# Output projection of a hybrid decoder layer by Strassen's scheme on pairs of row blocks, with the layer norm in steps between the products

## The chip, the cores and the metric

The kernel runs on 1 core of one Trainium2 chip. The metric is the device time of one execution in microseconds (us); a run of the kernel before was timed three times. PE is TensorE, DVE VectorE, ACT ScalarE, POOL GpSimd and SP SyncE, which issues the DMAs here.

## The reference, cut to what matters

One decoder layer on 4096 rows of 1024 columns in float32. One input projection feeds two branches of 512 columns each: sliding-window attention (`out_a`) and gated linear attention (`out_b`). Both are joined, projected by `w_out` (1024 x 1024), added to the input and normalised:

```
proj = jnp.einsum('bsd,de->bse', x, w_in[layer])
...
mix = jnp.einsum('bse,ed->bsd', jnp.concatenate([out_a, out_b], axis=-1), w_out[layer])
x = layer_norm(ALPHA * x + mix, ln_g[layer], ln_b[layer])
```

`layer_norm` takes mean and variance over the 1024 columns of a row, then multiplies by `ln_g` and adds `ln_b`.

## The kernel before

The rows are cut into 32 blocks of 128. Three stages follow each other on one core. **Stage A** projects a block for the attention branch, runs the sliding-window attention and writes the branch's transposed output (`att`, 128x512) to DRAM (`mixd[n][0]`). **Stage B** does the same for the linear-attention branch: per block the projections `bq`, `bv`, `bk`, `bg`, then the chunked recurrence. `b_state` (L537 to L553) scales the running state `tot` by a decay into `st` (DVE, L546) and splits it into `sbh` (ACT, L550) and `sbl` (POOL, L551); the products of `b_out` (L658 to L660) need both. `b_sums` forms `qp` on POOL (L532), which `b_turn` transposes (`tb`, L564). `b_store` (L680 to L687) transposes the block's output, copies it (`mb`) and writes it to `mixd[n][1]`. **Stage C** is the output projection and the layer norm.

All large products are made from float32 operands split in a high and a low part, so that one product is three matmuls: high by high, high by low, low by high. `split` (L97 to L105) makes the parts, ACT the high one (L100, a cast), DVE or POOL the low one (L105, a subtract). `project` (L127 to L137) issues the three matmuls of each of the 8 pieces of the contraction (lines L135, L136, L137), 128x512 each.

Per block stage C loads the two halves of the mix (`mr`) and the input rows (`xr`), splits `mr` into `mh`, `ml`, and makes two halves of 24 matmuls into PSUM (`py`). DVE reads each half (L761), takes its statistics (L762, L763) and works out the scale (L785 to L790, with two short ACT steps, and L776); ACT normalises the 128x1024 tile (L777), POOL multiplies by `ln_g` (L778), DVE adds `ln_b` (L779), and SP writes the rows out. The last block takes a shorter way (L771 to L773).

The program is written block by block, but a tile scheduler sets the order of the instructions on each engine from the tiles' dependences; an engine then works through its list in that order and waits at each instruction for its inputs and for its output's place to come free. Where a list puts an instruction that waits ahead of one that could go, the second waits too. SP's list of DMA issues is such a list as well. The output weights `w_o` are loaded and split at the last block of stage B (`load_group`, L112 to L121) into the places of the input weights.

## Time and profile before

| what | value |
|---|---|
| median of 3 runs | 1723.22 us (1723.13 to 1724.64) |
| the profiled execution's own time | 1724.99 us |
| its span | 1723.3 us |
| mean granted TensorE clock | 0.996 |
| PE busy | 1691.6 us, 98% |
| DVE busy | 1122.5 us, 65% |
| ACT busy | 774.2 us, 45% |
| POOL busy | 498.2 us, 29% |
| moved by DMA | 119.68 MB, mean 69 GB/s |

The span is the time from the first to the last instruction of one profiled execution; its busy shares are averages over the three stages, of which A ends at about 675 us, B at about 1358 us and C at the end. The granted clock is the share of TensorE's full speed that the throttle allowed: 1.00 is 2.4 GHz, and the lower of the two levels, 1.2 GHz, shows as a lower mean in a stretch.

### The profile page before, as it was taken

The page shows a single profiled execution, that of the slowest core. Times are in us where ns is not written, and L with a number is a line of the kernel's source. Part 1 is how long each engine was busy: PE and PEld are TensorE (multiplying, and loading weights), DVE is VectorE, ACT ScalarE, POOL GpSimd, SP SyncE. Part 2 cuts the span into 40 slices and gives each one's busy share as a digit, 9 for nine tenths or more (in the row PEclk, how much of TensorE's full clock was granted, in tenths as well). Part 3 has the DMA queues.
Part 4 walks back from the last instruction along what each step waited for, and adds up shares of the span by engine and source line. Part 5 has one row for each costly group of instructions (what it writes and reads, how often), then busy time and mean ns, then how long its engine had stood idle before and what let it go on. Part 6 is the DMA issues. An engine that isn't in the chain of part 4 may idle for free.

```text
span 1723.3 us, 26109 instructions
## 1 busy us (share of the span) xinstructions
PE 1691.6 (98%) x9466; PEld 1444.3 (84%) x9466; DVE 1122.5 (65%) x2547; ACT 774.2 (45%) x2064; POOL 498.2 (29%) x634
## 2 busy tenths in 40 slices
PE   7999999999999999999999999999999899999998
PEld 5788888888888887888888888888888788888886
DVE  6877777777777786666666666666665655555555
ACT  5444434444444455555555555555555522222221
POOL 3333322333222355222222222222222422222221
PEclk9999999999999999999999999999999899999999
DMA  6211111111111132111111111111111444444442
GB/s 197 80 38 37 37 46 47 37 38 38 37 53 40 37 102 79 50 38 38 38 38 38 38 38 38 38 38 38 38 37 38 153 146 143 142 144 146 147 147 86
DMA packets 65525, 119.68 MB, mean 69 GB/s; under 512 B 22642, under 2 KB 26100, under 8 KB 65396
## 3 DMA queue, kind: packets, MB, share of 16 engines
q1 hardware_dynamic: 65396, 118.01, 21.2%
q8 instruction: 74, 1.21, 0.3%
q14 instruction: 55, 0.45, 0.1%
HBM read 84.37 MB, written 33.62 MB: 68 GB/s over the span
## 4 chain that ended last, share of the span: by engine, by line
PE 58%; DVE 1%; ACT 1%; issue 0%; DMA 0%; POOL 0%; DVEq 0%; POOLq 0%; ACTq 0%
PE py L135 7%; PE py L137 7%; PE py L136 7%; PE bg L135 3%; PE bg L137 3%; PE bg L136 3%; PE bv L135 3%; PE bv L136 3%; PE bv L137 3%; PE bq L135 2%; PE bq L136 2%; PE bq L137 2%; PE bk L137 2%; PE bk L136 2%; PE bk L135 2%; PE to L684 1%
## 5 line engine op out<-in xcount | busy, mean ns | idle before, releaser
L361 POOL TENSOR_SCALAR_AFFINE_SELECT p<-hl 128x512 fp32r<-128x512 f32 x256 | 165.6, 682 | 382.7 <-ACT hl L355 348.8
L135 PE MATMUL py<-wh,mh 128*128 128x512 f32 x512 | 200.3, 391 | 0.0
L136 PE MATMUL py<-wl,mh 128*128 128x512 f32 x512 | 200.1, 391 | 0.0
L137 PE MATMUL py<-wh,ml 128*128 128x512 f32 x512 | 200.1, 391 | 0.0
L330 ACT ACTIVATE pr<-psc,ngm 128x128 f32<-128x128 f32 x256 | 90.7, 367 | 193.8 <-PE psc L311 138.1
L778 POOL TENSOR_TENSOR y<-y,lg 128x1024 f32<-128x1024 f32 x31 | 74.2, 2394 | 269.0 <-ACT y L777 253.5
L532 POOL TENSOR_TENSOR qp<-bqs,ee 128x256 f32<-128x256 f32 x32 | 23.6, 738 | 337.3 <-ACT ee L529 323.9
L137 PEld LDWEIGHTS py<-wh,ml 128*128 128x128 f32 x512 | 96.7, 189 | 20.3
L135 PEld LDWEIGHTS py<-wh,mh 128*128 128x128 f32 x512 | 96.7, 189 | 20.0
L136 PEld LDWEIGHTS py<-wl,mh 128*128 128x128 f32 x512 | 96.7, 189 | 19.8
L135 PE MATMUL pq<-wh,xh 128*128 128x512 f32 x256 | 105.0, 410 | 7.4 <-ACT wh L100 6.3
L135 PE MATMUL pg<-wh,xh 128*128 128x512 f32 x256 | 110.5, 433 | 0.1
L135 PE MATMUL bg<-wh,xh 128*128 128x512 f32 x256 | 107.0, 418 | 0.0
L137 PE MATMUL pq<-wh,xl 128*128 128x512 f32 x256 | 102.6, 401 | 1.2 <-DVE xl L105 1.2
L135 PE MATMUL bv<-wh,xh 128*128 128x512 f32 x256 | 103.5, 404 | 0.0
L100 ACT CAST mh<-mr 128x1024 fp32r<-128x1024 f32 x32 | 33.7, 1054 | 154.2 <-PE py L136 154.2
L105 DVE TENSOR_TENSOR xl<-xraw,xh 128x512 fp32r<-128x512 f32 x128 | 94.7, 760 | 11.6 <-ACT xh L100 5.2
L136 PE MATMUL pq<-wl,xh 128*128 128x512 f32 x256 | 102.1, 399 | 0.1
L136 PE MATMUL pg<-wl,xh 128*128 128x512 f32 x256 | 100.6, 393 | 1.3 <-POOL wl L105 1.0
L137 PE MATMUL pg<-wh,xl 128*128 128x512 f32 x256 | 101.0, 395 | 0.0
L136 PE MATMUL bv<-wl,xh 128*128 128x512 f32 x256 | 100.9, 394 | 0.0
L137 PE MATMUL bg<-wh,xl 128*128 128x512 f32 x256 | 100.7, 393 | 0.0
(221 smaller groups left out, 4907.1 us busy)
## 6 DMA issues: line engine op xcount, KB each, us to landing
xraw<-in_xt_dram SPq DMA_DIRECT2D x64, 512.0 KB
mr<-mx SPq DMA_DIRECT2D x64, 256.0 KB
xr<-in_xn_dram SPq DMA_DIRECT2D x32, 512.0 KB
out_dram<-y SPq DMA_DIRECT2D x31, 512.0 KB
mx<-att SPq DMA_DIRECT2D x32, 256.0 KB
mx<-mb SPq DMA_DIRECT2D x32, 256.0 KB
wraw<-in_w_a_dram SPq DMA_DIRECT2D x16, 256.0 KB
wraw<-in_w_b_dram SPq DMA_DIRECT2D x16, 256.0 KB
```

Source lines behind the costliest of these rows:

```text
L100: act.copy(hdst, src)
L105: leng.tensor_tensor(ldst, src, hdst, ALU.subtract)
L135: pe.matmul(dst[:, :n], a, hs[k][:, :n], start=(k == 0), stop=False)
L136: pe.matmul(dst[:, :n], a, ls[k][:, :n], start=False, stop=False)
L137: pe.matmul(dst[:, :n], b, hs[k][:, :n], start=False, stop=(k == NK - 1))
L330: act.activation(pr[:, i], sc[i], AF.Exp, bias=ngm[:, h : h + 1], scale=0.125, accum_out=den[:, h : h + 1])
L361: pool.affine_select(o, hl[:, i], [[0, 4], [sg_, P]], ALU.is_gt if b else ALU.is_ge, 0.0, base=0, channel_multiplier=-sg_,)
L532: pool.tensor_tensor(qp, B[n]["q"], ee, ALU.mult)
L684: pe.transpose(to[:, hs], og[:, hs], ident)
L778: pool.tensor_tensor(y, y, lg, ALU.mult)
```

## The change

Two blocks make a pair. Let `a11`, `a21` be the halves of the two blocks that come from stage A (even block, odd block) and `a12`, `a22` those from stage B. Instead of the eight half-products of 12 matmuls for a pair, seven products of sums and differences are made (the Strassen-Winograd form): 7 products of 4 pieces by 3 matmuls, 84 for a pair where there were 96.

The seven left operands of a pair are kept in DRAM (`opd[p][0..6]`). Four of them are sums, made on DVE in `b_store` of the odd block (L702, L704, L707, L709 of the changed kernel, 128x512 each). The seven combinations of `w_o` are made by `w_prepare` in small pieces during stage B, split there, written to DRAM (`wod`) and fetched by `w_fetch` at the turn from B to C: 28 tiles of 512 KB, where before 16 tiles of 256 KB were read. The `q` and `k` weights of stage B become one group of 528 columns, and some buffers of stage B lose their second copy or share a place (`gw`, `og`, `qp`, `kp`, `r0`).

In stage C `step(p, t)` makes product t of pair p into one of three PSUM banks (a, b, a, c, a, b, a), and DVE reads the bank after each product; a product that adds to a bank cannot begin before that read. Operands are loaded two pairs ahead and split one pair ahead, one between two steps (`split_op`, L855 and L856). `normed` is the layer norm of one block as a generator that is pushed on between the products: statistics, scale, `Identity` on ACT (L901), the multiplication by `ln_g` on POOL in two halves (L904), then the addition of `ln_b` in two halves (L908), on POOL for an even block, on DVE for an odd one. Pairs 0 and 1 are interleaved, the others go one by one. The small products of the scale have a scalar operand in place of a second tile.

```diff
--- before.py
+++ after.py
...
-    mixd = [
-        [dr.tile([P, 4, P], F32, tag=f"mx{n}_{h}", name=f"mx{n}_{h}") for h in range(2)]
-        for n in range(NB)
+    opd = [
+        [dr.tile([P, 512], F32, tag=f"op{p}_{i}", name=f"op{p}_{i}") for i in range(7)]
+        for p in range(NB // 2)
+    ]
...
+            p, odd = divmod(n, 2)
+            a2 = b1.tile([P, 512], F32, tag=f"mb{odd}", name=f"mb{n}")
+            act.copy(a2, to)
+            sp.dma_start(opd[p][4 + odd], a2)
+            if not odd:
+                a11 = b1.tile([P, 512], F32, tag="a11", name=f"a11_{p}")
+                a21 = b1.tile([P, 512], F32, tag="a21", name=f"a21_{p}")
+                sp.dma_start(a11, opd[p][0])
+                sp.dma_start(a21, a21d[p])
+                B[n]["a"] = a11, a21, a2
+                return
+            a11, a21, a12 = B[n - 1]["a"]
+            dve.tensor_tensor(a11, a11, a21, ALU.subtract)
+            sp.dma_start(opd[p][2], a11)
+            dve.tensor_tensor(a21, a21, a2, ALU.add)
+            sp.dma_start(opd[p][3], a21)
+            s2 = b1.tile([P, 4, P], F32, tag="om", name=f"s2_{p}").rearrange("p a s -> p (a s)")
+            dve.tensor_tensor(s2, a2, a11, ALU.subtract)
+            sp.dma_start(opd[p][1], s2)
+            dve.tensor_tensor(a12, a12, s2, ALU.subtract)
+            sp.dma_start(opd[p][6], a12)
...
+        def w_prepare(k, c):
+            q = []
+            for i in range(2):
+                for j in range(2):
+                    r = wr.tile([P, 256], F32, tag="wraw", name=f"wo{k}_{c}{i}{j}")
+                    sp.dma_start(r, w_o[k + 4 * i, :, 512 * j + 256 * c : 512 * j + 256 * c + 256])
+                    q.append(r)
...
+            def part(i, src):
+                w = b2.tile([P, 2, 256], F32R, tag="wo", name=f"wop{i}_{k}{c}")
+                split(w[:, 0], w[:, 1], src, act, dve)
+                sp.dma_start(wod[i][k][:, :, 256 * c : 256 * c + 256], w.bitcast(F32))
+            yield
+            part(0, r11)
+            dve.tensor_tensor(r11, r12, r11, ALU.subtract)
+            yield
+            dve.tensor_tensor(r12, r22, r12, ALU.subtract)
+            part(6, r22)
...
+        def op_places(p):
+            a = xp.tile([P, NK, P], F32, tag="xraw", name=f"oa{p}").rearrange("p a s -> p (a s)").bitcast(F32R)
+            b = xp.tile([P, NK, P], F32R, tag="xh", name=f"ob{p}").rearrange("p a s -> p (a s)")
+            c = xp.tile([P, NK, P], F32R, tag="xl", name=f"oc{p}").rearrange("p a s -> p (a s)")
+            w = {0: (b[:, LO], a[:, LO]), 3: (b[:, HI], a[:, HI]), 1: (c[:, LO], c[:, HI])}
+            for i in w:
+                op_load(p, w, i)
+            return w
+        PLACE = {0: (0, 0), 3: (0, 4), 1: (1, 0), 4: (1, 4), 2: (2, 0), 6: (2, 4)}
+        def w_fetch(i, pool_=None):
+            for k in range(4):
+                if pool_ is None:
+                    slot, k0 = PLACE[i]
+                    w = wp.tile([P, 2, 528 if slot == 1 else 512], F32R, tag=f"w{slot}_{k0 + k}", name=f"wo{i}_{k}")
+                else:
+                    w = pool_.tile([P, 2, 512], F32R, tag=f"wo{k}", name=f"wo{i}_{k}")
+                sp.dma_start(w[:, :, :512].bitcast(F32), wod[i][k])
+                wo[i][k] = w
...
             if last:
-                wo[0] = load_group(wr, w_o, 0, 512, 0, 512)
+                w_fetch(0)
+                w_fetch(3)
+            next(prep, None)
             pk = bank("pj", f"bk{n}")
-            project(pk, x, wb["k"], 256)
+            project(pk, x, wb["qk"], 256, off=272)
+            if last:
+                w_fetch(1)
+                w_fetch(4)
...
+            next(prep, None)
             if last:
-                wo[1] = load_group(wr, w_o, 512, 512, 2, 512)
+                ops = [op_places(p) for p in range(2)]
+                w_fetch(2)
+                w_fetch(6)
+            if n == NB - 2:
+                for _ in prep:
+                    pass
...
+        def op_more(p, w, which=(4, 2, 6, 5)):
+            for i in which:
+                h = c2.tile([P, 512], F32R, tag=f"oh{i}", name=f"oh{i}_{p}")
+                l = c2.tile([P, 512], F32R, tag=f"ol{i}", name=f"ol{i}_{p}")
+                w[i] = h, l
+                op_load(p, w, i)
...
+        def split_op(w, i):
+            h, l = w[i]
+            act.copy(h, l.bitcast(F32))
+            dve.tensor_tensor(l, l.bitcast(F32), h, ALU.subtract)
+        def product(dst, w, i, more=False):
+            h_, l_ = w[i]
+            for k in range(4):
+                h, l = wo[i][k][:, 0, :512], wo[i][k][:, 1, :512]
+                a, b = h_[:, k * P : (k + 1) * P], l_[:, k * P : (k + 1) * P]
+                pe.matmul(dst, a, h, start=(not more and k == 0), stop=False, skip_group_check=more)
+                pe.matmul(dst, a, l, start=False, stop=False, skip_group_check=more)
+                pe.matmul(dst, b, h, start=False, stop=(k == 3), skip_group_check=more)
...
+        def normed(n, y, st, late, tail):
...
+            dve.bn_aggr(mv, st.rearrange("p a b -> p (a b)"))
+            dve.tensor_scalar(ms, ms, 1.0, EPS, ALU.mult, ALU.add)
+            log_(rs, ms)
+            act.activation(rs, rs, AF.Exp, scale=-0.5)
+            yield
+            dve.tensor_scalar(nt, rs, rs, -0.5, ALU.mult, ALU.mult)
+            dve.tensor_scalar(nt, nt, ms, 1.5, ALU.mult, ALU.add)
+            dve.tensor_scalar(r2, nt, rs, None, ALU.mult)
+            rows = slice(n * P, (n + 1) * P)
+            if tail:
+                for s in (LO, HI):
+                    dve.scalar_tensor_tensor(y[:, s], y[:, s], mv[:, 0:1], lg[:, s], ALU.subtract, ALU.mult)
+                    dve.scalar_tensor_tensor(y[:, s], y[:, s], r2, lb[:, s], ALU.mult, ALU.add)
+                    sp.dma_start(out[rows, s], y[:, s])
+                return
...
+            nb_ = c2.tile([P, 1], F32, tag=f"nb{n % 2}", name=f"nb{n}")
+            dve.tensor_scalar(nb_, mv[:, 0:1], r2, -1.0, ALU.mult, ALU.mult)
+            act.activation(y, y, AF.Identity, bias=nb_, scale=r2)
+            yield
+            for s in (LO, HI):
+                pool.tensor_tensor(y[:, s], y[:, s], lg[:, s], ALU.mult)
+            if late is dve:
+                yield
+            for s in (LO, HI):
+                late.tensor_tensor(y[:, s], y[:, s], lb[:, s], ALU.add)
+            sp.dma_start(out[rows, :], y)
...
+        for p in range(2):
+            op_more(p, ops[p])
+        ys = [load_rows(p) for p in range(2)]
+        w_fetch(5, c1)
...
-            for i in range(2):
-                s = slice(512 * i, 512 * i + 512)
-                py = bank(("pj", "tp")[n % 2], f"py{n}_{i}")
-                project(py, (mh, ml), wo[i], 512)
-                dve.scalar_tensor_tensor(y[:, s], xr[:, s], ALPHA, py, ALU.mult, ALU.add)
-                dve.bn_stats(st[:, i, :], y[:, s])
...
-            dve.scalar_tensor_tensor(nb_, mv[:, 0:1], -1.0, rs, ALU.mult, ALU.mult)
-            act.activation(y, y, AF.Identity, bias=nb_, scale=rs)
-            pool.tensor_tensor(y, y, lg, ALU.mult)
-            dve.tensor_tensor(y, y, lb, ALU.add)
...
+        for i in ORDER:
+            for p in range(2):
+                split_op(ops[p], i)
+        pairs, later = NB // 2, []
+        def run_later():
+            for g in list(later):
+                if next(g, 0) == 0:
+                    later.remove(g)
...
+        STEPS = (("a", 0, False), ("b", 3, False), ("a", 1, True), ("c", 4, False), ("a", 2, True), ("b", 6, True), ("a", 5, True))
+        READS = ((0, 0, True), (1, 1, True), (0, 1, True), (0, 0, False), (1, 1, False), (0, 1, False), (1, 0, True))
+        state = {}
+        def step(p, t):
+            if t == 0:
+                b = {x: bank(g, f"p{x}{p}") for x, g in (("a", "pj"), ("b", "c"), ("c", "d"))}
+                st = [c2.tile([P, 2, 6], F32, tag=f"st{i}", name=f"cst{2 * p + i}") for i in range(2)]
+                state[p] = b, st
+            b, st = state[p]
+            x, op, more = STEPS[t]
+            product(b[x], ops[p], op, more)
+            i, half, first = READS[t]
+            y, s = ys[p][i], (LO, HI)[half]
+            if first:
+                dve.scalar_tensor_tensor(y[:, s], y[:, s], ALPHA, b[x], ALU.mult, ALU.add)
+            else:
+                dve.tensor_tensor(y[:, s], y[:, s], b[x], ALU.add)
+            if t in (3, 4, 5, 6):
+                dve.bn_stats(st[i][:, half, :], y[:, s])
+            run_later()
+            if t in (5, 6):
+                g = normed(2 * p + i, y, st[i], (pool, dve)[i], p == pairs - 1 and i == 1)
+                next(g)
+                later.append(g)
...
+        for group in [(0, 1)] + [(p,) for p in range(2, pairs)]:
+            for t in range(7):
+                for p in group:
+                    step(p, t)
+                    if p + 2 < pairs and t == 2:
+                        ops[p + 2] = op_places(p + 2)
+                    elif p + 2 < pairs and t > 2:
+                        op_more(p + 2, ops[p + 2], ORDER[t : t + 1])
+                nxt = group[-1] + 1
+                if nxt == pairs:
+                    continue
+                if t == 4:
+                    ys[nxt] = load_rows(nxt)
+                ready = range(7)[t : t + 1] if nxt > 2 else ((), (), (), (), (0, 1, 2), (3,), (4, 5, 6))[t]
+                for i in ready:
+                    split_op(ops[nxt], ORDER[i])
+        while later:
+            run_later()
```

**VectorE, stage B, block 20.** `am` is the masked attention tile of the block, `st` the scaled state, `r4` a small helper of the next block, `al` a low part, `tot` the running state, `a11`, `a21` the operands of the pair before. Before:

```order
L630 TENSOR_TENSOR gw20_13066<-bg20_12996,nrm_396 128x512
L590 COPY_PREDICATED am0_7814<-cs_373,pat20_13095 128x512
L546 TENSOR_SCALAR st20_13110<-tot19_12890,dd20_13107 128x128 x2
L482 TENSOR_TENSOR r41_399<-bq21_13082,r41_399 128x2x16
L105 TENSOR_TENSOR al20_13104<-am0_7814,ah20_13103 128x512
L612 TENSOR_TENSOR tot20_13144<-pu20_13137,st20_13110 64x256 x2
```

The change:

```order
L595 COPY_PREDICATED am0_7810<-cs_441,pat20_13372 128x512
L546 TENSOR_TENSOR dd20_13384<-sm20_13277,sm19_13010 128x2
L702 TENSOR_TENSOR a11_10_13563<-a11_10_13563,a21_10_13564 128x512
L488 TENSOR_TENSOR r41_467<-bq21_13359,r41_467 128x2x16
L112 TENSOR_TENSOR al20_13381<-am0_7810,ah20_13380 128x512
L551 TENSOR_SCALAR st20_13387<-tot19_13148,dd20_13384 128x128 x2
L617 TENSOR_TENSOR tot20_13421<-pu20_13414,st20_13387 64x256 x2
```

`st` stood right behind `am`; now the subtract of a pair's operands, the helper and the low part `al` stand between them. The same order is there in blocks 6, 8, up to 28; in the odd blocks `st` stands behind `am` and `dd` as before.

**VectorE, stage C, end of pair 8 and begin of pair 9** (blocks 16 to 19). `pa9` and `pb9` are banks of pair 9, `ol`, `oh` low and high parts of operands of the next pair, `nb` and `cnt` scale terms, `y17` the odd block of pair 8. Before, around the same block:

```order
L761 SCALAR_TENSOR_TENSOR y16_17354<-xr16_17348,py16_0_17357 128x512
L779 TENSOR_TENSOR y15_17273<-y15_17273,lb_16046 128x1024
L762 BN_STATS cst16_17355<-y16_17354 128x6
L761 SCALAR_TENSOR_TENSOR y16_17354<-xr16_17348,py16_1_17384 128x512
L762 BN_STATS cst16_17355<-y16_17354 128x6
```

The change:

```order
L948 SCALAR_TENSOR_TENSOR y18_17978<-y18_17978,pa9_18044 128x512
L856 TENSOR_TENSOR ol5_10_18040<-ol5_10_18040,oh5_10_18039 128x512
L889 TENSOR_SCALAR cnt17_18033<-crs17_18032 128x1
L890 TENSOR_SCALAR cnt17_18033<-cnt17_18033,mv17_18031 128x1
L891 TENSOR_SCALAR cr217_18034<-cnt17_18033,crs17_18032 128x1
L900 TENSOR_SCALAR nb17_18070<-mv17_18031,cr217_18034 128x1
L948 SCALAR_TENSOR_TENSOR y19_17980<-y19_17980,pb9_18045 128x512
L908 TENSOR_TENSOR y17_17806<-y17_17806,lb_16481 128x512 x2
L948 SCALAR_TENSOR_TENSOR y18_17978<-y18_17978,pa9_18044 128x512
L856 TENSOR_TENSOR oa11_18108<-oa11_18108,ob11_18109 128x512 x2
L950 TENSOR_TENSOR y18_17978<-y18_17978,pc9_18046 128x512
```

The addition of `ln_b` to `y` of the block before (L779) stood between the two reads of a block; it now stands as L908 ahead of the second read of bank `pa9`. The same is there for the ends of pairs 2, 4, 5, 7, 8, 10, 11, 13 and 14; at the other ends L908 stands right behind that read.

**SP, the turn from stage B to stage C.** `wo` are the weights of stage C, `sd31` and `sm31` the two ends of a small transfer through DRAM that the state of block 31 needs, `ol4_0` an operand of pair 0, `y0` the input rows of block 0. Before:

```order
L520 DMA sd31_164<-r031_15840 1x256
L521 DMA sd31_164<-r131_15841 1x256
L687 DMA mx30_1_130<-mb30_15861 128x512
L112 DMA wraw2_4_15932<-in_w_o_dram 128x512
L112 DMA wraw2_5_15938<-in_w_o_dram 128x512
L524 DMA sm31_15846<-sd31_164 128x4x1
```

The change:

```order
L781 DMA wo4_2_16228<-wod4_2_215 128x2x512
L781 DMA wo4_3_16230<-wod4_3_216 128x2x512
L526 DMA sd31_256<-r031_16242 1x256
L527 DMA sd31_256<-r131_16243 1x256
L693 DMA op15_4_178<-mb30_16261 128x512
L760 DMA oc1_16320<-op1_1_77 128x512
L781 DMA wo2_0_16324<-wod2_0_205 128x1024
L530 DMA sm31_16248<-sd31_256 128x4x1
...
L760 DMA ol4_0_16441<-op0_4_73 128x512
...
L872 DMA y0_16464<-in_xn_dram 128x1024
```

`sd31` stood behind 13 weight tiles of 256 KB; it now stands behind 16 of 512 KB, one more of them stands between it and `sm31`, and 25 further transfers stand ahead of the input rows of block 0.

## Rows read from the trace of the kernel before

**Rows 1.** The page's first part: busy time, share of the span, instructions.

```profile
PE 1691.6 (98%) x9466; PEld 1444.3 (84%) x9466; DVE 1122.5 (65%) x2547; ACT 774.2 (45%) x2064; POOL 498.2 (29%) x634
```

**Rows 2.** The chain that ended last, shares of the span.

```profile
PE 58%; DVE 1%; ACT 1%; issue 0%; DMA 0%; POOL 0%; DVEq 0%; POOLq 0%; ACTq 0%
```

**Rows 3.** Windows: from:to, length, busy us of PE PEld DVE ACT POOL, PEclk, DMA, GB/s.

```profile
750.00:1300.00 550.00, 550.00 (x3421) 485.40 (x3420) 333.09 (x796) 302.55 (x743) 139.81 (x178) 1.00 0.13 38
1410.00:1700.00 290.00, 290.00 (x1281) 240.14 (x1280) 158.34 (x322) 73.00 (x108) 63.36 (x27) 1.00 0.42 143
```

**Rows 4.** Timeline of PE, stage C: start, length (us), engine, line, operation.

```profile
1700.03 0.39 PE L135 MATMUL py<-wh,mh 128*128 128x512 f32 x1
1700.26 0.39 PE L136 MATMUL py<-wl,mh 128*128 128x512 f32 x1
```

**Rows 5.** Timeline of DVE, stage C: first reads of two blocks, one block between.

```profile
1590.07 0.69 DVE L761 SCALAR_TENSOR_TENSOR y<-xr,py 128x512 f32<-128x512 f32 x1 [1.34 <-PE py L137]
...
1611.83 0.69 DVE L761 SCALAR_TENSOR_TENSOR y<-xr,py 128x512 f32<-128x512 f32 x1 [1.35 <-PE py L137]
```

**Rows 6.** Groups of stage C, 1410 to 1700 us: busy us, mean ns, idle before.

```profile
L761 DVE SCALAR_TENSOR_TENSOR y<-xr,py 128x512 f32<-128x512 f32 x54 | 37.1, 687 | 68.1 <-PE py L137 68.1
...
L779 DVE TENSOR_TENSOR y<-y,lb 128x1024 f32<-128x1024 f32 x26 | 31.9, 1226 | 45.5 <-POOL y L778 45.5
...
L778 POOL TENSOR_TENSOR y<-y,lg 128x1024 f32<-128x1024 f32 x27 | 64.6, 2394 | 229.1 <-ACT y L777 229.1
...
L777 ACT ACTIVATE y<-y,nb,crs 128x1024 f32<-128x1024 f32 x27 | 33.6, 1244 | 21.9 <-DVE nb L776 21.9
```

**Rows 7.** Groups of stage B, shapes apart: a POOL multiply.

```profile
L636 POOL TENSOR_TENSOR gw<-gw,gs 128x512 f32<-128x512 f32 x26 | 33.7, 1298 | 75.2 <-ACT r L481 75.2
```

**Rows 8.** Timeline of one block of stage B: DVE, ACT, POOL, PE.

```profile
1074.60 0.73 DVE L590 COPY_PREDICATED am<-cs,pat 128x512 f32<-128x512 uint32 x1
1075.22 1.19 DVE L546 TENSOR_SCALAR st<-tot,dd 128x128 f32<-128x128 f32 x2
...
1076.43 0.68 DVE L105 TENSOR_TENSOR al<-am,ah 128x512 fp32r<-128x512 f32 x1
...
1076.44 0.83 ACT L550 CAST sbh<-st 64x256 fp32r<-64x256 f32 x2 [0.46 <-DVE st L546]
...
1074.83 1.30 POOL L636 TENSOR_TENSOR gw<-gw,gs 128x512 f32<-128x512 f32 x1 [2.89 <-ACT r L481]
1076.92 1.59 POOL L551 TENSOR_TENSOR sbl<-st,sbh 64x256 fp32r<-64x256 f32 x2 [0.80 <-ACT sbh L550]
...
1078.69 0.28 PE L659 MATMUL bo<-sbl,bth 128*128 128x256 f32 x1
```

**Rows 9.** Timeline of DVE and POOL, turn from B to C.

```profile
1362.73 1.77 DVE L105 TENSOR_TENSOR al<-am,ah 128x512 fp32r<-128x512 f32 x1
...
1362.36 1.60 POOL L636 TENSOR_TENSOR gw<-gw,gs 128x512 f32<-128x512 f32 x1 [1.36 <-ACT gs L629]
```

**Rows 10.** Windows of the turn, and of the start.

```profile
1345.00:1410.00 65.00, 60.35 (x259) 48.39 (x258) 40.57 (x81) 25.18 (x51) 20.30 (x14) 0.92 0.45 152
1370.00:1375.00 5.00, 5.00 (x17) 3.92 (x16) 3.48 (x12) 1.04 (x3) 0.00 (x0) 0.66 0.59 238
5.00:10.00 5.00, 3.30 (x6) 1.74 (x6) 3.45 (x7) 3.01 (x6) 1.84 (x2) 1.00 0.91 318
```

**Rows 11.** Timeline of PE at the turn, waits in brackets.

```profile
1342.18 0.39 PE L137 MATMUL bv<-wh,xl 128*128 128x512 f32 x1
...
1349.53 1.26 PE L684 MATMUL to<-cs,og 128*128 128x128 f32 x4 [1.89 <-DVE og L674]
...
1366.84 0.79 PE L658 MATMUL bo<-sbh,bth 128*128 128x256 f32 x2 [1.33 <-ACT sbh L550]
```

**Rows 12.** Timeline of the end: last matmul and last write.

```profile
1714.76 0.39 PE L137 MATMUL py<-wh,ml 128*128 128x512 f32 x1
...
1719.50 0.99 SPq L773 DMA_DIRECT2D out_dram<-y  x2
```

More of the change, by code (lines that the diff above doesn't have):

```diff
@@ new lines, in w_all, with op_load @@
+        def w_all():
+            for k in range(4):
+                for c in range(2):
+                    yield from w_prepare(k, c)
+        prep = w_all()
+        wo = [[None] * 4 for _ in range(7)]
+        LO, HI = slice(0, 512), slice(512, 1024)
+        def op_load(p, w, i):
+            sp.dma_start(w[i][1].bitcast(F32), opd[p][i])
+        def op_places(p):
[6 more added lines that the diff above has]
+            return w
```

112 lines of the change are left out of this document (57 added, 55 removed).

## The prediction

> **What bounds the kernel now.** I read the busy shares of the profile's page first: PE is busy 98% of the span, no other engine over 65% [rows 1]. The chain of waits says the same, with PE far ahead of all others [rows 2]. Shares over three stages hide their limits, so the windows come next: from 750 to 1300 us (stage B) PE is busy 550.00 of 550.00 us, from 1410 to 1700 us (stage C) 290.00 of 290.00, at full clock, while DVE has 158 and POOL 63 of those 290 us [rows 3]. So in both stages PE alone sets the pace: a matmul saved is worth its pitch, and a wait put in front of PE costs its length. The timeline of stage C gives the pitch of a 128x512 matmul, 1700.26 - 1700.03 = 0.227 us [rows 4], and the time of two blocks, 1611.83 - 1590.07 = 21.76 us [rows 5], which is 96 x 0.2267. The question is whether the other engines keep up when a pair of blocks has only 84 x 0.2267 = 19.04 us.
>
> **The products removed.** 16 pairs lose 12 matmuls each: 192 x 0.2267 = -43.5 us, all of it on the bound engine.
>
> **The layer norm's chain in stage C.** This is where I expect the gain to go. Before, DVE stood waiting for POOL ahead of every L779 (45.5 us in 26 blocks [rows 6]); PE did not mind, since the next half-product went to another bank. Now the order puts the odd block's addition (L908) ahead of the read of bank a after the third product (L948), at 9 of the 14 pair ends from pair 2 on; the fifth product adds to that bank and cannot begin before that read. Queued behind L908 are also the splits of the next operands. Let T be the end of a pair's last matmul. The fifth product of the next pair is due at T + 4 x 12 x 0.2267 = T + 10.88. Its chain: the last read and the statistics give the scale at about T + 1.6 where nothing stands between and T + 4.4 where other reads and splits do (estimates from the 0.69 us of a read [rows 6]); Identity 1.24 [rows 6]; on POOL six halves (multiply and add of the even block, multiply of the odd one), each between 2.394 / 2 = 1.20 [rows 6] and 1.30, the 128x512 multiply of stage B [rows 7], so 7.2 to 7.8, of which I take 7.5; two additions on DVE 1.23 [rows 6]; the read 0.69; some 0.4 for handing over. From T + 1.6 that is T + 12.7, a wait of 1.8; from T + 4.4 it comes to T + 15.5, a wait of up to 4.8. Where L908 stands behind the read, 0.4 is left. As the order repeats after three pairs, I take 1.8 + 0.4 + 4.8 = 7.0 per three pairs, 2.35 each: 14 x 2.35 = +32.9 us. Bounds: 0, if the addition always comes in time, and 14 x 4.8 = 67.
>
> **The clock.** Behind a wait of 1.33 us at the turn [rows 11] the next windows were granted 0.66, a mix of 2.4 and 1.2 GHz, and PE got 17 matmuls into 5 us instead of 22 [rows 10]: 1.1 us lost, and some more in the stretch before. I take 1.6 for each of the five longest waits, +8; bounds 0 (no wait lowers it) and 14 x 1.6 = 22.
>
> **Stage B.** In the even blocks from 6 to 28 the state `st` now stands behind a new subtract and `al`. In the trace of before `st` began at 1075.22, right after `am`; `sbh` followed at 1076.44, `sbl` on POOL from 1076.92 to 1078.51, and the product that needs it began at 1078.69 [rows 8]: 0.18 us of slack. The new subtract (0.68, like `al`), the helper and `al` (0.68 [rows 8]) put `st` some 1.4 later, so PE waits about 1.2: 12 x 1.2 = +14.4 us. The lower bound is 0 (the list waits elsewhere anyway); the upper one adds a subtract that waits for POOL's `gw`: that ran until 1076.13 while the subtract is due at 1075.33 [rows 8], 0.8 more in 12 blocks, and so up to +24. The other three DVE operations of an odd block and their writes lie in the 40% of stage B in which DVE is idle [rows 3], at nothing; without that cover they cost at most 16 x 3 x 0.68 = 33, which the idle time speaks against. The weights' combinations sit in blocks 0 to 6: casts of some 0.41 (half of the two for `sbh` [rows 8]) that can stand ahead of a due one; I take +2, between 0 and 7 blocks x 2 x 0.41 = 6. The merged q and k weights and the shared buffers change no matmul count; a buffer that frees late would show as a PE wait in all blocks, and I take 0.
>
> **The turn from B to C.** Before, this stretch had 4.65 us without PE and a clock of 0.92 [rows 10], with waits of 1.89 and 1.33 [rows 11]. The splits of `w_o` that shared it are gone, so block 31 should be done some 4.8 us earlier (half of what idle time and clock cost there). Against that stand the transfers: from where the last weights of `bv` come free (its last matmul began at 1342.18 [rows 11]; I take 1341 for the first of the places) some 20 tiles of 512 KB, 18 of 256 KB and two of input rows, 16.3 MB, are ahead of pair 0's first read. At 318 GB/s, the most seen in a window [rows 10], that is 51 us, so 1392; the six products behind the first three steps need the banks read and take 6 x 2.72 = 16.3, and with about 2 for the reads and the clock pair 2 begins near 1410.4. That is where the fourth block ended before (1715.0 - 28 x 10.88). So the 5.4 us that pairs 0 and 1 save are given back: +5.4. Bounds: -3 (the transfers are hidden and block 31 is early) and, at the 238 GB/s seen there [rows 10], 17 us later, +22. For pair 2, whose additions find POOL with two pairs at once, +2 (0 to 5).
>
> **The end.** The last write was issued 4.7 us after the last matmul began [rows 12]. Now the block before the last one still has its four halves on POOL (5.0) behind the last products: +2.7; bounds 0 and 5.
>
> **Sum.** -43.5 + 32.9 + 8 + 14.4 + 2 + 5.4 + 2 + 2.7 = +23.9 us. The profiled execution took 1724.99 us (span 1723.3), 1.8 over the median of 1723.22; so 1748.9 for it and **1747** for the median.
>
> **A rule against the change.** At 1362.73 a 128x512 subtract on DVE took 1.77 us where it takes 0.68 elsewhere, and it ended 0.54 us after the POOL multiply beside it did [rows 8, 9]. So DVE operations with two tiles in SBUF can stand still behind POOL. The Trainium skill, page "SBUF — State Buffer", section "Who interferes with whom", names the port pair that the two engines share as an exclusive lock, and its section "SBUF: two separate sides" counts a DVE operation with two SBUF inputs among those that take it; by that rule, the trace agrees; it would make the time that of the first rival below. Before, such pairs hardly met in stage C: POOL had one multiply a block, and DVE waited for it. Now a pair has seven splits and two additions of that kind on DVE (9 x 0.68 = 6.1 us) against 7.5 us on POOL.
>
> **The rivals.**
> - *Locked out.* If some 2 us of these meet inside each chain of the nine pairs, and 0.8 in each even block of B, +18 and +9.6 come on top: about 1775. For it speaks the one row of 1.77; against it, that DVE has over 4 us of slack in a pair.
> - *The chain fits* (the other side). If scale, Identity, POOL and the additions are through in 10.88 us, PE runs stage C without a wait: the terms 32.9, 8 and 2 go, 1704. It decides at 10.88 - 1.6 - 1.24 - 1.23 - 0.69 - 0.4 = 5.7 us for six POOL halves, 0.95 each; the rows say 1.20 at least, but the order could also let the even block's additions slip behind. Where the delay of `st` is hidden too, 1690.
> - *Stage B hides its delay.* `sbl` is late but PE finds its other products first: without 14.4, 1733. Against it: PE has its own fixed order and 0.18 us of slack.
> - *Nothing gained or lost.* The waits come to half of what I take and the clock stays up: 1723.
> - That the products are not saved is excluded by the order: 1344 matmuls where there were 1536.
>
> **How the numbers follow.** Forecast 0.52 (own range 1733 to 1763), locked out 0.12, chain fits 0.18 (0.12 at 1704, 0.06 at 1690), stage B hides 0.12, nothing 0.06. A range from 1704 to 1772 leaves out the 1690 case, about half of the one at 1775 and some of that at 1704, 0.16 in all. Over 0.2% (3.4 us, about what a measurement of this kernel tells from no change) faster: the third case and a little of the last, 0.20; within: 0.06; slower: 0.74.
>
> **What would show it.** Right: in a window of stage C after the turn PE is busy about 89% with 21.4 us for a pair; PE's idle time before the fifth product (L864 into bank a) is put down to DVE's L948, DVE's before L908 to POOL's L904; in stage B every second block takes some 22.8 instead of 21.55 us, with PE waiting for `sbl`; some windows of stage C show a clock under 1.00. Wrong: PE at 100% in stage C and 19.04 us a pair (the chain fits); blocks of stage B all at 21.55; subtracts on DVE or halves on POOL well over their 0.68 and 1.30 (locked out).

## The result: slower by 4.6%, over three times what was forecast

| what | before | after |
|---|---|---|
| median of 4 runs each | 1723.90 us | 1803.16 us (1801.89 to 1804.98) |
| ratio, 95% interval | 1 | 1.0461 (1.0448 to 1.0474) |
| profiled execution's span, mean clock | 1723.3 us, 0.996 | 1800.4 us, 0.980 |

The forecast was 1747 us, 1704 to 1772: right in its direction, 56 us short. The profile's page of the changed kernel, busy shares and the shares of the chain of waits (before: [rows 1, 2]):

```profile
PE 1684.3 (94%) x9274; PEld 1419.7 (79%) x9274; DVE 1261.6 (70%) x2814; ACT 811.3 (45%) x2176; POOL 554.1 (31%) x685
...
PE 27%; DVE 11%; DMA 8%; POOL 6%; issue 4%; ACT 4%; SPq 1%; POOLq 0%; DVEq 0%; ACTq 0%
```

PE is no longer busy all the time, and only 27% of the chain runs over it. Windows of the changed kernel: most of blocks 0 to 6 of stage B, its later blocks, pairs 2 to 15 of stage C, and two of 5 us behind one wait each (before: [rows 3]):

```profile
core 0: us, PE busy (x) PEld busy (x) DVE busy (x) ACT busy (x) POOL busy (x), PEclk, DMA share, GB/s
720.00:850.00 130.00, 124.55 (x741) 106.06 (x741) 104.00 (x249) 76.54 (x201) 32.44 (x37) 1.00 0.54 175
850.00:1300.00 450.00, 436.75 (x2689) 381.70 (x2689) 291.74 (x661) 238.65 (x582) 119.11 (x141) 1.00 0.21 71
1451.70:1786.30 334.60, 290.57 (x1177) 230.98 (x1175) 223.17 (x447) 95.66 (x174) 118.69 (x90) 0.94 0.46 157
1541.00:1546.00 5.00, 5.00 (x12) 3.93 (x13) 2.93 (x5) 1.33 (x3) 0.00 (x0) 0.53 0.97 357
1564.50:1569.50 5.00, 5.00 (x22) 4.14 (x23) 3.26 (x5) 0.65 (x2) 0.00 (x0) 1.00 0.84 305
```

Neither stage B nor stage C is at PE's pace any more. To split the 77.1 us of span (1800.4 - 1723.3), I take fixed places of the program from PE's timeline: the first transpose (`to`, L689) of blocks 0, 6 and 29, the first matmul of pair 2, and one pitch behind the start of the last.

| stretch | before | after | difference | forecast |
|---|---|---|---|---|
| start to block 0 | 698.9 | 704.4 | +5.5 | 0 |
| blocks 0 to 6 | 129.5 | 142.3 | +12.8 | +2 |
| blocks 6 to 29 | 495.9 | 515.1 | +19.2 | +14.4 |
| block 29 to pair 2 | 86.1 | 89.9 | +3.8 | 0 (+5.4, less 5.4 saved) |
| pairs 2 to 15 | 304.6 | 334.6 | +30.0 | +4.8 |
| last matmul to the end | 8.3 | 14.1 | +5.8 | +2.7 |

Pairs 2 to 15 split further: 168 matmuls less, 168 x 0.2267 = -38.1; PE idle, 334.6 - 290.57 = +44.0 (forecast 32.9 + 2); and 290.57 us for 1176 matmuls that take 266.6 at full clock, +24.0 (forecast 8). Not all of the 24.0 is the clock: the last matmul before each of the 21 waits counts its whole 0.39 us instead of the pitch of 0.227, some 3.4 us together. The rest fits the granted clock: a mean of 0.94 over 334.6 us stands for some 40 us at half speed, and so for 20 us lost (an estimate from the third row).

**Stage C.** The waits of pairs 2 to 15 (total, times, longest, in us): PE,

```profile
PE pa L864 <- DVE y L948: 28.6, 13, 4.6
PE pa L864 <- DVE y L950: 7.0, 4, 2.2
PE pa L864 <- ACT ob L855: 6.7, 3, 3.1
PE pa L864 <- DVE cnt L889: 1.6, 1, 1.6
```

and DVE:

```profile
DVE y L908 <- POOL y L904: 51.6, 15, 4.7
```

One of them in the timeline (start, duration, instruction; in brackets the idle time before it and what ended it):

```profile
1536.59 2.49 POOL L904 TENSOR_TENSOR y<-y,lg 128x512 f32<-128x512 f32 x2
1536.67 0.34 SPq L909 DMA_DIRECT2D out_dram<-y  x1
1537.06 0.42 SPq L760 DMA_DIRECT2D oa<-op  x1
1537.90 2.33 DVE L908 TENSOR_TENSOR y<-y,lb 128x512 f32<-128x512 f32 x2 [4.71 <-POOL y L904]
1540.15 0.67 DVE L948 SCALAR_TENSOR_TENSOR y<-y,pa 128x512 f32<-128x512 f32 x1
...
1540.48 0.62 ACT L855 CAST ob<-oa 128x512 fp32r<-128x512 f32 x1 [6.04 <-DMA oa<-op]
...
1540.97 0.77 PE L864 MATMUL pa<-wo,oh 128*128 128x512 f32 x1 [4.63 <-DVE y L948]
```

This is the forecast's chain: DVE stands at L908 for POOL, the read L948 behind it, PE behind the read. But by PE's timeline it is not the fifth product alone that waits: the fifth waits 21.7 us for its read (7 times) and 6.7 for an operand (3), the third 8.5 (7) and the seventh 7.0 (4). Two more things show. ACT has waited 6 us for `oa`: on SP's queue the even block's write (L909), issued only once POOL is done, stands ahead of that load. And the two additions take 2.33 us where two take 1.23 [rows 6], beside POOL.

The window from 1541.00 lies behind this wait of 4.63 us: clock 0.53, 12 matmuls, the lower level of 1.2 GHz almost throughout. The one from 1564.50 lies behind a wait of 1.84: 1.00 and 22 matmuls.

**Stage B.** Blocks 1 to 6 took 23.94, 23.80, 24.00, 23.36, 23.61 and 23.60 us; then even blocks of 23.3 alternate with odd ones of 21.53. Lines of an even block in the timeline (before: [rows 8]):

```profile
1057.32 1.29 POOL L641 TENSOR_TENSOR gw<-gw,gs 128x512 f32<-128x512 f32 x1 [2.81 <-ACT r L487]
...
1057.71 0.92 DVE L546 TENSOR_TENSOR dd<-sm,sm 128x2 f32<-128x2 f32 x1
...
1058.55 0.68 DVE L702 TENSOR_TENSOR a<-a,a 128x512 f32<-128x512 f32 x1
...
1059.26 0.68 DVE L112 TENSOR_TENSOR al<-am,ah 128x512 fp32r<-128x512 f32 x1
...
1059.85 0.47 DVE L551 TENSOR_SCALAR st<-tot,dd 128x128 f32<-128x128 f32 x2
...
1060.84 1.54 POOL L556 TENSOR_TENSOR sbl<-st,sbh 64x256 fp32r<-64x256 f32 x2 [2.23 <-ACT sbh L555]
...
1062.43 0.39 PE L664 MATMUL bo<-sbl,bth 128*128 128x256 f32 x1 [0.75 <-POOL sbl L556]
```

The new subtract (L702) and `al` stand ahead of `st`, and PE waits for `sbl`, as forecast. Not forecast: `dd`, two columns wide, takes 0.92 us beside POOL's multiply (0.154 in the median of its 31). And `sbl` is only one of three waits of PE; from 850 to 1300 us, in ten even blocks:

```profile
PE bo L664 <- POOL sbl L556: 7.4, 10, 0.7
PE tb L569 <- POOL ee L537: 3.9, 11, 0.4
PE tr L495 <- DVE r L488: 1.9, 10, 0.2
```

The helper `r` stands behind L702 in DVE's list. `ee`, a POOL multiply of 128x256, takes 1.23 us in the even blocks, where the pair's subtracts L707 and L709 run beside it on DVE, and 0.74 in the odd ones (shortest, median, longest of 32, in ns):

```profile
L537 POOL TENSOR_TENSOR ee<-bqs,ee x32: 726/737/1227, 689.4 to 1387.3; 128x256 f32<-128x256 f32 x32
```

### The profile page after: what moved, and what is told of

Same layout as the page of the kernel before. It is cut to its first block, busy times and chain, and to the rows that moved or that the text cites. A ratio compares the mean times of both kernels' runs of the same rounds, so it can differ in the third digit from the quotient of the medians.

```text
span 1800.4 us, 26800 instructions
## 1 busy us (share of the span) xinstructions
PE 1684.3 (94%) x9274; PEld 1419.7 (79%) x9274; DVE 1261.6 (70%) x2814; ACT 811.3 (45%) x2176; POOL 554.1 (31%) x685
## 4 chain that ended last, share of the span: by engine, by line
PE 27%; DVE 11%; DMA 8%; POOL 6%; issue 4%; ACT 4%; SPq 1%; POOLq 0%; DVEq 0%; ACTq 0%
POOL y L904 3%; PE bv L144 2%; PE bv L143 2%; PE bv L145 2%; DMA ol<-op 2%; DMA a<-a 2%; PE bg L143 2%; PE bg L144 2%; PE bg L145 2%; DVE y L908 2%; PE bk L144 1%; PE bk L145 1%; PE bk L143 1%; POOL y L908 1%; DMA wod<-wop 1%
## 5 line engine op out<-in xcount | busy, mean ns | idle before, releaser
L904 POOL TENSOR_TENSOR y<-y,lg 128x512 f32<-128x512 f32 x62 | 84.2, 1380 | 265.7 <-ACT y L901 219.8
L143 PE MATMUL pg<-w,xh 128*128 128x512 f32 x256 | 110.6, 433 | 0.8 <-DVE vv L259 0.8
L143 PE MATMUL pq<-w,xh 128*128 128x512 f32 x256 | 104.1, 407 | 6.7 <-ACT w L107 6.3
L143 PE MATMUL bg<-w,xh 128*128 128x512 f32 x256 | 106.0, 414 | 0.0
L145 PE MATMUL pq<-w,xl 128*128 128x512 f32 x256 | 102.4, 400 | 2.3 <-DVE xl L112 2.3
L143 PE MATMUL bv<-w,xh 128*128 128x512 f32 x256 | 103.3, 404 | 0.0
L112 DVE TENSOR_TENSOR xl<-xraw,xh 128x512 fp32r<-128x512 f32 x128 | 93.1, 748 | 14.1 <-POOL xh L109 6.2
L144 PE MATMUL pq<-w,xh 128*128 128x512 f32 x256 | 101.7, 397 | 0.1
L144 PE MATMUL pg<-w,xh 128*128 128x512 f32 x256 | 100.7, 394 | 1.1 <-POOL w L112 0.8
L145 PE MATMUL pg<-w,xl 128*128 128x512 f32 x256 | 101.1, 395 | 0.0
L144 PE MATMUL bv<-w,xh 128*128 128x512 f32 x256 | 100.9, 394 | 0.0
L145 PE MATMUL bv<-w,xl 128*128 128x512 f32 x256 | 100.7, 393 | 0.0
L145 PE MATMUL bg<-w,xl 128*128 128x512 f32 x256 | 100.2, 392 | 0.0
L144 PE MATMUL bg<-w,xh 128*128 128x512 f32 x256 | 100.2, 391 | 0.0
L864 PE MATMUL pa<-wo,oh 128*128 128x512 f32 x128 | 56.2, 439 | 35.5 <-DVE y L948 21.8
L384 PE MATMUL po<-p,vv 128*128 128x512 f32 x252 | 79.8, 416 | 5.3 <-POOL p L369 4.7
```

Source lines behind the costliest of these rows:

```text
L112: leng.tensor_tensor(ldst, src, hdst, ALU.subtract)
L143: pe.matmul(dst[:, :n], a, hs[k][:, c], start=(k == 0), stop=False)
L144: pe.matmul(dst[:, :n], a, ls[k][:, c], start=False, stop=False)
L145: pe.matmul(dst[:, :n], b, hs[k][:, c], start=False, stop=(k == NK - 1))
L384: pe.matmul(po, vvs[n - b][:, g, :], parts.pop((g, b, i)).rearrange("p h s -> p (h s)"), start=(b == 0 and i == 0), stop=(b == 1 and i == 1),)
L864: pe.matmul(dst, a, h, start=(not more and k == 0), stop=False, skip_group_check=more)
```

## The experiments

`after(x, y)` in the kernel's code puts x behind y in the scheduler's lists and adds no semaphore. Each single time is beside a run of the kernel before on the same chip (1724 to 1725 us).

**e1 and e2: the addition behind a read.** The odd block's L908 is held behind the latest read of a bank (`latest[0]`): the one after the third product (e1), or, with two more `yield`s, after the fifth (e2).

```diff
             for s in (LO, HI):
-                late.tensor_tensor(y[:, s], y[:, s], lb[:, s], ALU.add)
+                add = late.tensor_tensor(y[:, s], y[:, s], lb[:, s], ALU.add)
+                if late is dve:
+                    after(add.ins, latest[0])
...
```

> The changed kernel with one order changed: the odd block's addition of ln_b on VectorE (L908) is held behind the read of bank a after the third product; nothing else differs. Theory A (VectorE stands at that addition for POOL, and TensorE waits for the read behind it): the waits of 1.9 to 4.6 us before the fifth product go, a smaller one of about 2 us before the seventh product stays (the fifth product's read is still behind the addition), a pair falls from 23.9 to about 21.5 us, the time to about 1770 us. Theory B (the operand loads are late on SP's queue, behind writes that wait for POOL): the splits of the next pair are still late, a pair stays at 23 to 24 us, the time within 10 us of 1803.

Measured: e1 1794.25 us. What PE waited for in pairs 2 to 15:

```profile
PE pa L864 <- DVE y L952: 22.5, 12, 2.6
PE pa L864 <- DVE y L950: 16.4, 10, 1.9
```

and DVE:

```profile
DVE y L908 <- POOL y L904: 45.0, 13, 4.2
```

The fifth product's wait moved to the seventh, behind the next read (L952), the third product waits more than before (L950), and DVE still waits for POOL at L908. So the forecast's idea, that one product per pair waits, is wrong: bank a is read after the first, third, fifth and seventh product, and each read that another product of the pair needs can be the late one. The time lies within 10 us of 1803, as theory B had it.

> As the run before, with the addition held one bank read further, behind the read after the fifth product. Theory A: no read that TensorE waits for is left behind POOL; a pair comes to 19.0 to 19.8 us, the clock of stage C back to over 0.98, the time to about 1740 us (14 pairs less 4.2 to 4.9). Theory B: a pair at 22 us or more, time over 1775 us.

Measured: e2 1775.38 us, at the edge of theory B. DVE no longer waits at L908, but has a new wait in front of the reads. Its largest, in pairs 2 to 15, and PE's:

```profile
DVE oa L856 <- ACT ob L855: 55.9, 17, 6.6
...
PE pa L864 <- DVE y L954: 19.6, 11, 3.2
```

and how one comes about, in e2's timeline:

```profile
1577.02 2.55 POOL L904 TENSOR_TENSOR y<-y,lg 128x512 f32<-128x512 f32 x2
1577.10 0.34 SPq L913 DMA_DIRECT2D out_dram<-y  x1
...
1577.53 1.22 SPq L760 DMA_DIRECT2D oa<-op  x2
...
1580.85 0.62 ACT L855 CAST ob<-oa 128x512 fp32r<-128x512 f32 x1 [5.97 <-DMA oa<-op]
...
1581.50 0.69 DVE L856 TENSOR_TENSOR oa<-oa,ob 128x512 fp32r<-128x512 f32 x1 [4.38 <-ACT ob L855]
```

The even block's write goes out when POOL has finished that block; the loads of the next operands leave right behind it; cast and split wait for them, and the split stands in DVE's list ahead of a due read. This is a second link, on SP's queue.

**e5 and e8: that write behind the loads.** e5 is e2 with the write behind the first operand loads of a later pair; e8 has this alone (the scheduler then puts L908 behind the read after the third product by itself at most pair ends, as in e1).

```diff
-            sp.dma_start(out[rows, :], y)
+            if late is pool:
+                yield
+                yield
+                yield
+            after(sp.dma_start(out[rows, :], y).ins, loads[-1])
```

> The kernel of the second run (addition behind the fifth product's read) with one more order changed: on SP's queue the even block's write, which waits for POOL, is held behind the first three operand loads of the next pair but one. If these late loads are what is left of stage C's loss (in the second run VectorE stood 56 us for ScalarE's casts of oa, which stood for the loads), a pair comes to 19.1 to 19.7 us for all pairs from 3 on, TensorE's clock in that stretch to 0.99 or more, and the time to about 1742 us (12 pairs less 22.2 to 19.4). If VectorE is simply too full, or the transfers too slow, a pair stays at 21 us or more and the time over 1762 us.

> The changed kernel with SP's order alone repaired (the even block's write behind the operand loads); the scheduler then puts the odd block's addition behind the third product's read, as in the first run, at every pair end. So it is the first run plus SP's order. If the late loads alone hold stage C back, a pair falls from 23.6 us (first run) to 19.5 us and the time to about 1750 us, as in the fifth run. If the addition ahead of the fifth product's read costs its own wait, a pair stays at 21 to 21.8 us by a wait of about 2 us before the seventh product, and the time at 1770 to 1780 us.

Measured: e5 1751.37, e8 1774.74 us. The window of e5 over pairs 3 to 14:

```profile
1482.40:1716.30 233.90, 231.16 (x1009) 188.76 (x1008) 195.72 (x385) 83.94 (x154) 110.29 (x72) 1.00 0.61 200
```

and PE's largest waits in e8, pairs 2 to 15:

```profile
PE pa L866 <- DVE y L956: 16.6, 10, 2.1
PE pa L866 <- DVE y L954: 8.0, 3, 4.2
```

With both links taken away PE is busy 231 of 234 us at full clock, and most pairs take 19.2 us. e8 came out as expected. The order on SP gives 19.5 us on top of e1 (1794.25 - 1774.74) and 24.0 on top of e2 (1775.38 - 1751.37); the addition's place gives 27.8 in e2 and 23.4 on top of e8. In e8 PE waits for reads behind the additions, in e2 for reads behind late operands; the third product's waits, 16.4 us in e1, are gone in e8, so they came from the late operands too. e5 also shows that the lower clock was a consequence: without the waits it stays at 1.00. e5 came out 9 us above what was expected: block 0 came 3.3 us later than in e2, three pairs took 20.0 to 20.6 us, and e2's pairs 3 to 14 had taken 21.8 on average, not the 22.2 that the expectation started from.

**e3: the subtracts of stage B.** The four pair operations are held behind the state update `tot` of the next-but-one block. The third now overwrites its input `a2`, where it took the place of `om` before.

```diff
-            dve.tensor_tensor(a11, a11, a21, ALU.subtract)
+            after(dve.tensor_tensor(a11, a11, a21, ALU.subtract).ins, tots[-1])
...
```

> The changed kernel with the four VectorE operations on a pair's operands (L702 to L709) held until the state update of the next but one block is made, where VectorE was idle for 2.1 us; s2 overwrites its input instead of sharing the place of om. Theory C (the subtract ahead of st, and the operations that lock POOL out at ee, cost the even blocks 1.77 us): blocks 6 to 30 come to 21.55 to 21.7 us each, the state of the turn is reached about 20 us earlier, time about 1783 us; the first six blocks keep part of their loss (the weights' pieces). Theory D (the extra writes or the buffers that lost their second copy delay the even blocks): they stay at 23 us or more, time 1800 us or more. If the four operations now delay om, every second block shows a wait before the transposes of om.

Measured: 1789.28 us, blocks 7 to 28 at 21.53 us (one at 21.83):

```profile
850.00:1300.00 450.00, 449.83 (x2802) 396.89 (x2801) 304.41 (x690) 247.22 (x607) 115.05 (x147) 1.00 0.22 73
```

Blocks 6 to 29 take 495.5 us, as in the kernel before (495.9), instead of 515.1: practically the whole loss there was the place of the four operations in DVE's list, not their work. `ee` is back at 0.74 in all blocks. (What the free place of `om` adds was not tried apart.) Blocks 0 to 6 took 2.9 us more than in the changed kernel, and the turn 3.9 more, probably because block 31's operands are now written later (not tried).

**e4: the weights' pieces,** two per block and behind `tot`.

```diff
-            next(prep, None)
             pk = bank("pj", f"bk{n}")
...
                 b_update(n - 1)
+                next(prep, None)
+                next(prep, None)
```

> The changed kernel with the 56 pieces of the combined output weights spread two to a block over stage B, each held behind the state update, instead of standing in the first seven blocks. Theory E (too much work at once on VectorE and ScalarE in blocks 0 to 6, ahead of operations that TensorE waits for): of the 12 us that blocks 1 to 6 lose, some 8 or more come back; blocks 7 to 28 gain nothing, and odd blocks stay at 21.55 us; time about 1792 us. Theory F (each piece costs its time wherever it stands): the loss moves to the later blocks, 0.2 us for a piece, and the time stays within 3 us of 1803.

Measured: 1799.29 us. Blocks 1 to 6 took 21.90, 23.60, 21.54, 23.60, 21.54, 23.60: 6.5 us less from block 0 to 6, but even blocks of 23.60 instead of 23.3 up to block 28, 3.5 more from block 6 to 29. So part of the loss came back and part moved, between theory E and theory F: the pieces cost time wherever they are put, though less when spread.

**e6, e7, e9: all orders together.** e6 is e5 with e3, the pieces four at a time in the blocks without subtracts, and the short end for both last blocks (first line below). e7 adds an order on SP at the turn, with `linked` (the recurrence's small transfers first, then rows, operands and weights as they are needed); e9 is e7 with another order of the pools, so that the first input rows need not wait for stage B's last buffers.

```diff
-                g = normed(2 * p + i, y, st[i], (pool, dve)[i], p == pairs - 1 and i == 1)
+                g = normed(2 * p + i, y, st[i], (pool, dve)[i], p == pairs - 1)
...
+    def linked(ins):
+        after(ins, chain[-1])
+        chain.append(ins)
```

> All repairs together: stage C as in the run before, the pair subtracts after the state update as in the third run, the weights' pieces four at a time in the blocks without those subtracts, and the short way at the end for both blocks of the last pair. If the losses are separate and add up: stage C 19.4 us a pair, blocks 1 to 30 of stage B at 21.55 to 21.8 us, the end 3 us shorter: 1803 - 62 - 18 - 10 - 3 = about 1710 us, 0.8% faster than the kernel before. If the gaps of stage B are used up by both (2.1 us for 2.5 us of pieces), blocks 2 to 28 go up by 0.5 to 1 us every second time and the time to about 1720 us. If the turn gets longer by what stage B gained (as it did in part in the third run), 1725 us or more.

> The kernel of the sixth run with the turn from stage B to C ordered on SP's queue: block 31's small transfer (sd, sm) ahead of the weight tiles that come after the first eight, the input rows and operands of pairs 0 and 1 each ahead of the weights of their product, the loads of pairs 2 and 3 behind all of these; the pools of stage C open in another order. Theory G (the turn is long since transfers that are due stand behind ones that are not): the wait of 7.8 us for the state of block 31 and that of 10.7 us for the first operand of the fourth product go, pair 2 begins near 1410 instead of 1433, the time comes to 1695 to 1703 us, 1.2 to 1.7% under the kernel before. Theory H (the turn is bound by its 16 MB at some 330 to 400 GB/s, 41 to 49 us from 1347 on, however they are ordered): the waits move to other products, pair 2 begins at 1425 or later and the time stays above 1712 us.

> The seventh run with the input rows of stage C in the places that stage B leaves first. In the seventh run TensorE stood 8.1 us at the third product for VectorE's read, that for the rows of block 0, and their loads for the last writes of pair 15's operands. If that order is what is left of the turn, the wait falls under 3 us, and the time to about 1709 us, 0.9% under the kernel before. If the transfers of the turn are bound by their bytes, the wait moves to a later product and the time stays at 1714 to 1718 us.

Measured: e6 1721.53 us, ratio 0.9979 (0.9969 to 0.9989); e7 1716.43, 0.9958 (0.9944 to 0.9972); e9 1714.05, 0.9942 (0.9925 to 0.9959). e6 came out as its second case: blocks 2 to 28 take some 0.5 us more every second time. With every stage mended the turn is what is left: e6's largest PE waits there,

```profile
PE pc L877 <- DMA ol<-op: 10.7, 1, 10.7
PE bo L665 <- ACT sbh L555: 7.8, 1, 7.8
```

and a window of 50 us of it:

```profile
1350.00:1400.00 50.00, 33.26 (x167) 26.67 (x165) 24.79 (x53) 16.91 (x40) 5.75 (x7) 0.84 0.91 331
```

The DMA engines are busy 91% at 331 GB/s: earlier work only waits for its operands there. e7's order took the 7.8 down to 1.1 and turned the other into 8.1 us for a read whose input rows left late; e9's left 4.3 of that. Pair 2 began at 1428.1 us in e7 and 1426.3 in e9: both fit the theory that the turn is bound by its bytes, and the better orders gave 5.1 and 2.4 us.

**e10 and e11: stage B's q and k weights in two groups again,** in the changed kernel (e10) and in e9 (e11), since block 0 was late and nothing so far said why.

```diff
-                wb["qk"] = load_group(wr, w_b, 0, 528, 1, 528)
+                wb["q"] = load_group(wr, w_b, 0, 272, 1, 272)
+            if n == 2:
+                wb["k"] = load_group(wr, w_b, 272, 256, 3, 256)
```

> The changed kernel with the q and k weights of stage B again in two groups (q loaded and split near the end of stage A, k at its third block, into places of their own); at the turn to stage C the two halves of a weight tile then come by two DMAs of 256 KB into those places. No computation is left out. Theory M (the late merged group of 528 columns costs the 5.5 us by which the first block of stage B was late): the first block transpose on PE, at 698.9 us in the kernel before and 704.4 in the changed one, comes at 698 to 700; the rest as in the changed kernel, some 1798 us. Theory N (the delay comes from elsewhere, the first block's own work or how the scheduler's lists fall): it stays between 702 and 706, time 1801 to 1806.

> The same edit on top of e9 (all orders repaired), whose first block transpose came at 701.3 us. Theory M: at 698 to 700, and the time falls by 1.5 to 3 us to about 1711.5 to 1712.5, unless the eight more DMAs at the turn to stage C take it back. Theory N: within 1 us of 701.3, and 1713.5 to 1716.

Measured: e10 1798.49 us, its block 0 at 701.1; e11 1710.95 us (1709.82 to 1712.63), ratio 0.9920 (0.9904 to 0.9937), block 0 at 699.3. The stretch of 35 us at the end of stage A, of the changed kernel:

```profile
625.00:660.00 35.00, 28.65 (x150) 22.93 (x150) 30.18 (x58) 21.00 (x55) 21.78 (x23) 0.95 0.43 137
```

and of e10:

```profile
625.00:660.00 35.00, 30.47 (x172) 24.20 (x170) 29.80 (x63) 22.07 (x63) 21.61 (x27) 1.00 0.40 125
```

The two groups cost PE nothing there: clock 1.00 and 1.8 us more of PE's work in the stretch. In the ten kernels with the merged group block 0 came between 701.3 and 706.0, so single pairs of runs tell its price only roughly: 3.3 us by e10, 2.0 by e11 against e9. e10's 701.1 lies between the two theories' ranges, e11's 699.3 fits theory M. The 2.2 that e10 leaves are down to 0.4 in e11 with the other orders mended; which of those did it was not tried.

## Why the prediction was wrong in size

The forecast of the span was short by 53.2 us (77.1 - 23.9): 25.2 in pairs 2 to 15, 10.8 in blocks 0 to 6, 5.5 ahead of block 0, 4.8 in blocks 6 to 29, 3.8 at the turn and 3.1 at the end. Every stretch came out longer than forecast; the direction was right for the reasons given, the sizes were not.

**"The layer norm's chain in stage C."** The chain is there, row for row; the step that failed is that only "the fifth product" would wait, in a repeat of three pairs that comes to 2.35 us a pair. The fifth product's read cost less than the 32.9 us put down for it, 21.7, and no wait was over 4.63; but the third and the seventh product, which had no term, waited 15.5, and operands that came late 6.7. In all PE was idle 44.0 us for a forecast of 34.9. (Two roundings in the working, 4.8 where 15.5 - 10.88 is 4.6 and 2.35 where 7.0 / 3 is 2.33, change little.) The write on SP's queue that delays the next operands was not looked at, though it is worth nearly as much as the addition: 24 of the 51.8 us that both orders give.

**"The clock": +8, measured some 20.** I took 1.6 us for each of five waits. There were 21 waits, and though not each lowered the clock (the one of 1.84 us did not), the lower level held for some 40 us in all. A wait of 4.63 was followed by 5 us at 0.53, which costs 10 matmuls, 2.3 us, in these alone. The +24.0 of PE's busy time holds 3.4 more that are the ends of matmuls before a wait.

**"The weights' combinations": +2, measured +12.8 in those blocks.** I priced a cast of 0.41 on ACT, twice a block, and put nothing down for DVE's subtracts. e4 took 6.5 us of it back; the other 6.3 lie in every second block, three times 2.05, as in the even blocks further on. Some 1.77 of each 2.05 are the pair's operations, which I had counted from block 6 only, so about 7.5 of the 12.8 are the pieces (an estimate, 12.8 - 3 x 1.77). Moving the pieces moves their cost: with both orders mended (e6) blocks 0 to 29 still take 634.6 us against 625.4 before, +9.2, and PE's waits there are for a split on DVE (`lal`, 4.6 us in 11 waits from 850 to 1300).

**"Stage B": +14.4, measured +19.2.** Right in kind; 1.77 us per even block instead of 1.2. But the wait for `sbl`, the whole of the forecast's 1.2, is only 0.74; the rest are `ee` (0.39), `r` (0.19) and the ends of matmuls before the three waits. The step that failed is that "the other three DVE operations" cost "nothing" since DVE is idle 40% of the time: two of them slow POOL's `ee`, and PE waits for it. e3 confirms that the place is the cause: 19.6 us back in blocks 6 to 29.

**"The turn from B to C" and "the end".** The turn took +3.8 for a forecast of 0 net; PE's largest waits there are 8.7 us for the cast of an operand of the fourth product and 4.4 for the state of block 31, where the forecast had pair 0's first read wait for its input rows. The end took +5.8 for 2.7, over its bound of 5: POOL's four halves of the block before the last took 3.13 and 3.37 us a pair instead of 2.5, and DVE's last steps beside them 2.41 and 2.68:

```profile
1788.54 2.41 DVE L895 SCALAR_TENSOR_TENSOR y<-y,mv,lg 128x512 f32<-128x512 f32 x2
1788.94 3.13 POOL L904 TENSOR_TENSOR y<-y,lg 128x512 f32<-128x512 f32 x2 [12.75 <-ACT y L901]
...
1791.61 2.68 DVE L896 SCALAR_TENSOR_TENSOR y<-y,cr,lb 128x512 f32<-128x512 f32 x2
1792.04 3.37 POOL L908 TENSOR_TENSOR y<-y,lb 128x512 f32<-128x512 f32 x2
```

**The merged q and k weights, for which I took 0:** 2 to 3 us (e10, e11). I had looked for a buffer that frees late. That the splits come all at once is the likely reason; it was not tried apart.

**The rivals.** "Locked out" was real as a mechanism, but no more than a part. Of the 30 L908 on DVE in the changed kernel, 15 lie beside POOL and take 1.76 us, the others 0.68; in e2 (L910) none lies beside POOL, and all take 0.68:

```profile
L908 DVE TENSOR_TENSOR y<-y,lb x30: 674/1206/1773, 1465.1 to 1776.7; 128x512 f32<-128x512 f32 x30
...
L910 DVE TENSOR_TENSOR y<-y,lb x30: 672/679/689, 1472.3 to 1756.1; 128x512 f32<-128x512 f32 x30
```

The Trainium skill, page "SBUF — State Buffer", section "Who interferes with whom", has such DVE and POOL operations exclude each other; the trace agrees with these two numbers. But e2 takes this away together with the wait for POOL, so its 28 us do not tell the two apart. What speaks against the rival is e5: there the splits of `oa` take 1.41 us in the mean (second line), where they took 0.68 in the changed kernel (first line), and a pair still takes 19.2 us.

```profile
L856 DVE TENSOR_TENSOR oa<-oa,ob 128x512 fp32r<-128x512 f32 x24 | 16.2, 683 | 0.7 <-ACT ob L855 0.5
...
L858 DVE TENSOR_TENSOR oa<-oa,ob 128x512 fp32r<-128x512 f32 x22 | 30.2, 1410 | 1.0 <-ACT ob L857 0.3
```

"The chain fits" was wrong for the order as it stood and right for the engines: e5 shows that their work goes into such a pair. "Stage B hides its delay" was wrong: +19.2 us.

**Where the products' gain is.** e11, the best version, beats the kernel before by 13.6 us of span, 0.8% of the time. Pairs 2 to 15 take 274.8 us, 29.8 less; block 0 gives back 0.4, blocks 0 to 29 9.3, the turn 4.8 and the end 1.7. So of 43.5 us of products a third is left, and that only after the orders are mended.

## What to carry to other kernels

Matmuls taken from the engine that bounds are worth their time only if everything queued for it still comes in time: go through the list of each engine, the one that issues DMAs too, and ask of every instruction that will wait what stands behind it. A mean idle share covers nothing by itself; look at the block in which the work lands. And where a wait vanishes in one list, expect the next list's: here each of the two links was worth only about half. And work put into DVE's idle time can still slow POOL, and PE behind it.

## What was not expected of the hardware

A DVE operation of two columns (`dd`) took 0.91 to 0.98 us in the 13 of 31 cases in which it met a POOL multiply, and ended within 0.02 us of it each time; otherwise it took 0.15. POOL slows too: `ee` takes 1.23 us instead of 0.74 beside two subtracts, and its 128x512 multiply, 1.30 [rows 7], takes 1.748 in the median of e5, where DVE is busy 196 of 234 us:

```profile
L906 POOL TENSOR_TENSOR y<-y,lg x48: 1280/1748/1766, 1489.0 to 1708.6; 128x512 f32<-128x512 f32 x48
```

And DMA moved 331 GB/s over 50 us of e6's turn and 357 in 5 us of the changed kernel's stage C, where [rows 10] had shown 318 at the most.
